# Opening an encoder layer: the modulation by quarters instead of halves, w_in tiles split in two pieces, and turns of the identity on TensorE

## The chip, the cores and the metric

One core of one Trainium2 chip runs the whole layer in one launch. The metric is the device time of one execution in microseconds (us), median of several runs. Engines: TensorE (PE), VectorE (DVE), ScalarE (ACT), GpSimd (POOL), SyncE (SP, which issues most DMAs). PE's records come in two kinds, matmuls (a transpose is one, with the identity as the second operand) and weight loads (PEld).

## The reference, cut to what matters

One layer of an encoder over 1024 prompt rows and 32 sample rows of 1024 channels, all in float32. The change concerns the beginning:

```
ada = silu(c) @ w_ada + b_ada          # c: one row for the prompt, one for the sample
sh1, sc1, gt1, sh2, sc2, gt2 = split(ada, 6)
h = rms_norm(x, g_pre_mix) * (1 + sc1) + sh1
p = h @ w_in                            # 4256 columns: latents, q, k, v of branch B, two gates
```

Behind it come two kinds of attention (multi-head latent, and stick-breaking with a strict causal mask), gated and projected, and a feed-forward part with a causal convolution. Outputs are the rows y and the new cache rows and states.

## The kernel before, in words

Everything that PE multiplies has channels on the partitions, so the rows of x are transposed on their way in. `stage_h` (L335) makes h = shift + gain * normalised x in that form, as two parts, a rounded value hh (Hht) and a remainder hl (Hlt); a product with w_in is then three matmuls per tile of 128 channels, hh x wh, hl x wh and hh x wl (`mm3`, L72 to L74), where wh and wl are the same split of a weight tile (`hi` on ACT, L65; `lo` on DVE, L68). A w_in tile is 1024 channels x 128 columns, loaded by `wload` (L82). `w_in_tile` (L388) hands out a tile that was made ahead, if there is one in `in_w`.

`load` in `stage_h` brings one block of 128 rows (x), ACT sums its squares (L105), POOL makes the reciprocal root (L97, L98) and DVE scales the rows (L345). There are eight such blocks, and one tile xs with the 32 sample rows, laid as 128 partitions x 256 channels (`quarters`); its reciprocal root needs a matmul across partitions (`rstd_s`, L320 to L324).

Shift and scale of the first part are 2 x 1024 columns of w_ada. `ada_half` (L241) makes them for 512 channels: eight k-tiles of 128 input channels, each a DMA of 512 KB (L250) and four matmuls (L253) whose stationary operand is the silu of the two c rows, padded to 32 columns, so that four of them stand side by side in PE's columns; each streams 256 columns of w_ada. In the trace each counts as two PE instructions, so a k-tile is x8. The sums go to SBUF (L255), two transposes (L258, here called the turn) put channels on partitions, the bias is added (L261), and `gain` (L237) makes g * (1 + scale). Only then can ACT make h.

`norm_T` (L266) transposes four x blocks of one k-tile (128 channels) into one PSUM bank (L282), ACT writes f = gain * x + shift (L288), DVE makes hh (a cast, L291) and hl (L292). For blocks 4 to 7 and the first half of the channels, ACT writes hh too (`both`), and DVE casts nothing. The branch for sample rows (from L296) transposes xs anew at each call.

The order in `stage_h`: blocks 0 to 3, ada half 0, norm of blocks 0 to 3; mask; the first w_in tile (q, column 672); blocks 4 to 7; the second w_in tile (k); norm of blocks 4 to 7; the sample rows; ada half 1; and the second half of the channels for all. The engines' orders are worked out by a scheduler when the program is built: it takes each instruction by its data, its engine and its priority, so that transposes, ada k-tiles and w_in matmuls of the first q and k tile (`sb_pair`, L408, over three column blocks of 352) are mixed on PE. The order thus comes from the built program, not from the text of the code. Pools set what can be ahead: wada holds 8 buffers of w_ada tiles and of x, W holds 2 w_in tiles each raw, wh and wl; PSUM has eight banks, s (3), pv (1), tr (2), mm (2).

After the last w_in matmul of the first q and k tiles, the k tile is turned back to rows (`to_natural`, L404).

Of the kernel before, what the change touches and what calls it, by code (L numbers as in the profile page):

```python
# [8 lines left out]
F32 = mybir.dt.float32  # L9
F32R = mybir.dt.float32r  # L10
BF16 = mybir.dt.bfloat16
AF = mybir.ActivationFunctionType
ALU = mybir.AluOpType
# [4 lines left out]
P = 128  # L18
D = 1024
KT = 8  # L20
# [24 lines left out]
class K:  # L45
# [192 lines left out]
            out[:, k], self.adaT[:, v, k], 1.0, self.gvT[:, g0 + k0 : g0 + k0 + n].unsqueeze(2).broadcast_to([P, n, 2]),  # L238
            ALU.add, ALU.mult)

    def ada_half(self, hf, wp, tp):  # L241

        nc, a = self.nc, self.a
        acc = self.tl(tp, [P, 256], F32, f"ada{hf}")
        ps = self.bank("s")
        for k in range(KT):

            last = hf == 1 and k >= KT - 2
            w = self.tl(*((self.W, [P, 1024]) if last else (wp, [P, 2 * 512])), F32, "wr").rearrange("p (v n) -> p v n", v=2)
            nc.sync.dma_start(w, a["w_ada"][0, k * P : (k + 1) * P].rearrange("p (v h n) -> p v h n", v=6, h=2)[:, 0:2, hf])  # L250
            for j in range(4):
                c = (j % 2) * 256
                nc.tensor.matmul(ps[32 * j : 32 * j + 32, :256], self.cT[:, k], w[:, j // 2, c : c + 256],  # L253
                                 start=k == 0, stop=k == KT - 1)
        nc.vector.tensor_copy(acc, ps[:, :256])  # L255
        tr = self.bank("s")
        for c in range(2):
            nc.tensor.transpose(tr[:, c * P : c * P + P], acc[:, c * P : c * P + P], self.idt)  # L258
        for c in range(2):
            k = slice(4 * hf + c, 4 * hf + 4, 2)  # L260
            nc.vector.tensor_tensor(self.adaT[:, 0:2, k],  # L261
                                    tr[:, c * P : c * P + P].rearrange("p (v j r) -> p v j r", v=2, j=2)[:, :, :, 0:2],
                                    self.bT[:, :, k].unsqueeze(3).broadcast_to([P, 2, 2, 2]), ALU.add)
        self.gain(self.g1, 1, 0, 4 * hf, 4)


    def norm_T(self, t0, xs, g, sv, tp, k0=0, k1=KT):


        nc = self.nc  # L270
        if t0 < 8:
            n = len(xs) * P
            m = 512 // n
            c = slice(t0 * P, t0 * P + n)
            for k in range(k0, k1, m):
                tr = self.bank("tr")
                f = self.tl(tp, [P, 512], F32, "hf").rearrange("p (k c) -> p k c", k=m)
                for e in range(m):
                    kc = slice((k + e) * P, (k + e) * P + P)
                    for j, x in enumerate(xs):  # L280
                        o = e * n + j * P
                        nc.tensor.transpose(tr[:, o : o + P], x[:, kc], self.idt)  # L282
                h, l = self.Hht[:, k : k + m, c], self.Hlt[:, k : k + m, c]

                both = t0 == 4 and k0 == 0
                for e in range(m):
                    for x in (f, h) if both else (f,):
                        nc.scalar.activation(x[:, e], tr[:, e * n : e * n + n], AF.Identity,  # L288
                                             bias=self.adaT[:, sv, k + e, 0:1], scale=g[:, k + e, 0:1])
                if not both:  # L290
                    nc.vector.tensor_copy(h, f)  # L291
                nc.vector.tensor_tensor(l, f, h.bitcast(F32), ALU.subtract)  # L292
        else:
            tr = self.bank("tr")
            for c in range(2):
                nc.tensor.transpose(tr[:, c * P : c * P + P], xs[0][:, c * P : c * P + P], self.idt)  # L296
            f = self.tl(tp, [P, 512], F32, "hf")[:, :256].rearrange("p (k t) -> p k t", t=TS)
            for k in range(k0, k1):
                j, c = k // 2, k % 2
                nc.scalar.activation(f[:, k], tr[:, c * P + 32 * j : c * P + 32 * j + 32],  # L300
                                     AF.Identity, bias=self.adaT[:, sv, k, 1:2], scale=g[:, k, 1:2])
            f, h, l = (x[:, k0:k1] for x in (f, self.Hht[:, :, TP:T], self.Hlt[:, :, TP:T]))
            nc.vector.tensor_copy(h, f)
            self.lo(l, f, h)
# [29 lines left out]
    def stage_h(self):  # L334
        nc = self.nc  # L335
        self.new_H()
        a = self.a
        with self.tc.tile_pool(name="st_h", bufs=2, reuse_waits="tile") as tp, self.tc.tile_pool(name="wada", bufs=8, reuse_waits="tile") as wp:
            self.ada_prep(tp)
            xts = []  # L340

            def load(t):
                x = self.tl(wp, [P, D], F32, "x")
                nc.sync.dma_start(x, a["x_prompt"][0, t * P : (t + 1) * P])
                nc.vector.tensor_scalar(x, x, self.rstd(self.sumsq(x, P, tp, "jk0", 1024), D, P), None, ALU.mult)  # L345
                xts.append(x)

            def norm(t, hf):
                self.norm_T(t, xts[t : t + 4] if t < 8 else [xs], self.g1, 0, tp, 4 * hf, 4 * hf + 4)

            for t in range(4):
                load(t)
            self.ada_half(0, wp, tp)
            norm(0, 0)
            mk = self.tl(tp, [P, 272], F32, "mk")
            nc.gpsimd.dma_start(mk, a["k_mask"][:, P:])
            nc.vector.tensor_copy(self.msk, mk)
            w = [self.w_in_tile(672)]
            for t in range(4, 8):
                load(t)  # L360
            w.append(self.w_in_tile(672 + 512))
            self.in_w = w
            norm(4, 0)
            xs = self.tl(tp, [P, 256], F32, "xs")
            self.quarters(xs, a["x_sample"][0], nc.gpsimd)
            nc.gpsimd.dma_start(self.sel, a["k_sel"])
            self.ada_half(1, wp, tp)
            nc.vector.tensor_scalar(xs, xs, self.rstd_s(xs, tp), None, ALU.mult)
            norm(0, 1)
            norm(8, 0)  # L370
            norm(4, 1)
            norm(8, 1)


    def mtile(self, wh, wl, xh, xl, blocks, nk, tags="mm"):
# [1351 lines left out]
    def part(self, s, i):  # L1727
        return [x[:, 512 * i : 512 * i + 512].rearrange("p (k c) -> p k c", k=4) for x in s]
# [554 lines left out]
```

## Time and profile before

| | us |
|---|---|
| median of 3 runs | 1734.95 (1734.91 to 1735.09) |
| profiled execution | 1733.42 |
| its span (first to last instruction) | 1731.7 |
| PE busy, matmuls | 1691.4 |
| DVE, ACT, POOL busy | 1249.7, 994.5, 274.6 |
| mean granted clock of PE | 0.997 |

The profile is of one execution, slightly shorter than the median of the runs; 1.7 us lie around its span. "PE busy" is time in which a matmul is under way by its record; records overlap, as the array is a pipeline, so the pitch from one start to the next says more on a matmul's cost than its duration. A row of the timeline has the start, the busy time of the group, the engine and line, the operation, out<-in by the program's names, shapes, the count, and in brackets the idle time just before and what ended it. A row of the windows has the stretch, its length, busy time (and number of instructions) of PE, PEld, DVE, ACT and POOL, then the clock granted to PE as a share of full speed, the share of the DMA engines in use, and GB/s.

### The profile page before, as it was taken

Reading aid. Unit: us, or ns where it says so; the run is one execution under the profiler, and the core shown is the slowest. Engines: PE = TensorE matmul, PEld = TensorE weight load, DVE = VectorE, ACT = ScalarE, POOL = GpSimd, SP = SyncE. Lnnn points to the kernel's source line nnn. Section 1 sums busy time; section 2 is a strip of 40 time slices with the busy share of each in tenths; the row PEclk is TensorE's granted clock in tenths of the full one; section 3 lists DMA queues with packets and bytes.
Section 4 is the critical chain, followed back from the end, with each engine's and each line's share of the span. In section 5 each row is a group of like instructions: output and inputs, shape, how many; then the busy total and the mean of one; then the engine's idle time right before and its main releaser. Section 6 shows DMA issues by size and latency. Waiting matters only on the chain. (4 is left out here: it accounts for less than half of the span.)

```text
span 1731.7 us, 29842 instructions
## 1 busy us (share of the span) xinstructions
PE 1691.4 (98%) x11546; PEld 1540.8 (89%) x11546; DVE 1249.7 (72%) x2104; ACT 994.5 (57%) x1943; POOL 274.6 (16%) x521
## 2 busy tenths in 40 slices
PE   6999999999999999999999999999999999999998
PEld 3999998999999989989888779999999999977886
DVE  4696594693873587768785678877787787788456
ACT  4595694683872677767774277444454444544442
POOL 2211111111110011101100042221111111210013
PEclk9999999999999999999999999999999999999999
DMA  9343333333332222122245631524323323697743
GB/s 325 97 126 96 107 120 85 114 105 92 113 114 54 71 79 65 61 75 68 95 170 180 190 131 41 164 97 135 129 92 128 128 92 129 204 339 248 242 147 122
DMA packets 170142, 223.78 MB, mean 129 GB/s; under 512 B 12933, under 2 KB 117072, under 8 KB 170000
## 3 DMA queue, kind: packets, MB, share of 16 engines
q1 hardware_dynamic: 154336, 177.91, 32.5%
q0 software_dynamic: 15440, 43.88, 7.2%
q8 instruction: 91, 1.49, 0.3%
q14 instruction: 51, 0.42, 0.1%
q10 hardware_dynamic: 224, 0.09, 0.0%
HBM read 170.06 MB, written 51.25 MB: 128 GB/s over the span
## 5 line engine op out<-in xcount | busy, mean ns | idle before, releaser
L65 ACT ACTIVATE wh<-wr 128x1024 fp32r<-128x1024 f32 (+6 forms) x161 | 134.3, 844 | 252.1 <-PE s L1737 80.0
L68 DVE TENSOR_TENSOR wl<-wr,wh 128x1024 fp32r<-128x1024 f32 (+6 forms) x161 | 154.4, 967 | 148.0 <-ACT wh L65 147.7
L72 PE MATMUL mm<-hh,wh 128*128 128x352 f32 x696 | 231.7, 333 | 2.8 <-ACT nat L861 2.8
L73 PE MATMUL mm<-hl,wh 128*128 128x352 f32 x696 | 226.8, 326 | 0.4 <-DVE hl L292 0.4
L74 PE MATMUL mm<-hh,wl 128*128 128x352 f32 x696 | 225.8, 324 | 0.0
L72 PEld LDWEIGHTS mm<-hh,wh 128*128 128x128 f32 x696 | 131.2, 189 | 10.5 <-ACT nat L861 4.8
L73 PEld LDWEIGHTS mm<-hl,wh 128*128 128x128 f32 x696 | 131.4, 189 | 3.2 <-DVE hl L292 1.1
L74 PEld LDWEIGHTS mm<-hh,wl 128*128 128x128 f32 x696 | 131.5, 189 | 0.4 <-issue 0.4
L1738 PE MATMUL s<-T,wl 128*128 128x256 f32 (+1 forms) x328 | 93.6, 285 | 0.0
L1737 PE MATMUL s<-T,wh 128*128 128x256 f32 (+1 forms) x328 | 93.4, 285 | 0.0
L1736 PE MATMUL s<-T,wh 128*128 128x256 f32 (+1 forms) x328 | 93.3, 284 | 0.0
L1877 DVE SCALAR_TENSOR_TENSOR u<-u,c,u 128x1058 f32<-128x1058 f32 x68 | 87.0, 1317 | 1.9 <-ACT u L1874 0.7
L603 PE MATMUL tr<-c,A 128*128 128x128 f32 x576 | 83.4, 275 | 1.5 <-DVE PTl L68 0.8
L1736 PE MATMUL tr<-T,wh 128*128 128x272 f32 (+1 forms) x272 | 77.7, 286 | 0.0
L1738 PE MATMUL tr<-T,wl 128*128 128x272 f32 (+1 forms) x272 | 77.6, 285 | 0.0
L1737 PE MATMUL tr<-T,wh 128*128 128x272 f32 (+1 forms) x272 | 77.3, 284 | 0.0
L68 DVE TENSOR_TENSOR PTl<-tr,PTh 128x512 fp32r<-128x512 f32 x100 | 67.2, 683 | 11.9 <-ACT PTh L65 11.4
L603 PEld LDWEIGHTS tr<-c,A 128*128 128x128 f32 x576 | 66.4, 140 | 9.6 <-DVE PTl L68 1.7
L68 DVE TENSOR_TENSOR wl<-S,wh 128x1024 fp32r<-128x1024 f32 x40 | 48.9, 1223 | 35.0 <-ACT wh L65 35.0
L1738 PE MATMUL mm<-T,wl 128*128 128x256 f32 (+1 forms) x256 | 72.9, 286 | 0.3 <-DVE wl L68 0.2
L1736 PE MATMUL mm<-T,wh 128*128 128x256 f32 (+1 forms) x256 | 73.0, 285 | 0.0
L1737 PE MATMUL mm<-T,wh 128*128 128x272 f32 (+1 forms) x256 | 72.7, 284 | 0.0
(689 smaller groups left out, 5519.4 us busy)
## 6 DMA issues: line engine op xcount, KB each, us to landing
wr<-in_w_ada_dram SPq DMA_DIRECT2D x48, 512.0 KB, 4.4
wr<-in_w_up_dram SPq DMA_DIRECT2D x44, 512.0 KB, 4.5
dr<-in_w_down_dram SPq DMA_DIRECT2D x43, 512.0 KB, 6.4
wr<-in_w_in_dram SPq DMA_DIRECT2D x33, 512.0 KB, 4.8
wr<-gdn SPq DMA_DIRECT2D x30, 512.0 KB, 4.2
gdn<-u POOLq DMA_DIRECT2D x23, 512.0 KB, 5.2
gd<-nat POOLq DMA_DIRECT2D x48, 176.0 KB, 2.2
t<-gd SPq DMA_DIRECT2D x16, 528.0 KB, 6.0
```

The costliest lines, as they stand in the source:

```text
L65: self.nc.scalar.activation(out, in_, AF.Identity, scale=scale)
L68: return self.nc.vector.tensor_tensor(out, full, hi.bitcast(F32), ALU.subtract)
L72: m(ps, lh, rh, start=start, stop=False)
L73: m(ps, lh, rl, start=False, stop=False)
L74: self.pe = m(ps, ll, rh, start=False, stop=stop).ins
L603: self.nc.tensor.transpose(tr[:, (2 * s + q) * P : (2 * s + q + 1) * P], at[q][:, b * P : b * P + P], self.idt)
L1736: m(ps[:, :n], w[0][:, k], x[0][:, k, c], start=first and k == 0, stop=False, skip_group_check=True)
L1737: m(ps[:, :n], w[0][:, k], x[1][:, k, c], start=False, stop=False, skip_group_check=True)
L1738: i = m(ps[:, :n], w[1][:, k], x[0][:, k, c], start=False, stop=k == 3, skip_group_check=True)
L1877: nc.vector.scalar_tensor_tensor(y, u[:, w : w + YW], self.cvT[:, w, cc : cc + 1], y, ALU.mult, ALU.add)
```

## The change

The first part of ada is made in four quarters of 256 channels instead of two halves. A quarter has eight DMAs of 256 KB (pieces of 1 KB instead of 2 KB) and 8 x 4 matmuls of 128 columns, one transpose as its turn, and its sums lie in the one bank of pv instead of s. The order is: blocks 0 to 3, quarter 0, their norm for its two k-tiles; q weight tile; blocks 4 to 7; k weight tile; their norm for quarter 0; the sample rows, transposed once and kept (xT); then for quarters 1 to 3: ada and the norms of all rows.

The two w_in tiles are split in two pieces: 256 columns (the first two k-tiles) first, the other 768 after the norm of blocks 4 to 7.

ACT no longer writes hh for blocks 4 to 7; DVE casts as for the others.

`keep_busy` issues transposes of the identity into a bank that nobody reads: 15 after quarter 0's turn, and 5 each after the transposes of blocks 4, 5 and 6 in the second k-tile of quarter 0 (the table STANDS).

```
-    def ada_half(self, hf, wp, tp):
+    def keep_busy(self, ins, n):
+        for i in range(n):
+            with self.tc.issue_after(ins):
+                ins = self.nc.tensor.transpose(self.idle[:, i % 4 * P : i % 4 * P + P], self.idt, self.idt).ins
+
+    STANDS = {(4, 1, 0): 5, (4, 1, 1): 5, (4, 1, 2): 5}
+
+    def ada_quarter(self, q, wp, tp):
...
-        acc = self.tl(tp, [P, 256], F32, f"ada{hf}")
-        ps = self.bank("s")
-        for k in range(KT):
...
+        acc = self.tl(tp, [P, P], F32, "ada")
+        ps = self.bank("pv")
+        for kk in range(KT // 2):
...
+            for e in range(2):
+                k = 2 * kk + e
+                nc.sync.dma_start(w[:, e], a["w_ada"][0, k * P : (k + 1) * P].rearrange("p (v h n) -> p v h n", v=6, h=4)[:, 0:2, q])
+                for j in range(4):
+                    c = (j % 2) * P
+                    nc.tensor.matmul(ps[32 * j : 32 * j + 32, :P], self.cT[:, k], w[:, e, j // 2, c : c + P],
+                                     start=k == 0, stop=k == KT - 1)
+        nc.vector.tensor_copy(acc, ps[:, :P])
+        tr = self.bank("pv")
+        m = nc.tensor.transpose(tr[:, :P], acc, self.idt)
+        if q == 0:
+            self.keep_busy(m.ins, 15)
...
+        self.gain(self.g1, 1, 0, 2 * q, 2)
...
-                        nc.tensor.transpose(tr[:, o : o + P], x[:, kc], self.idt)
+                        ins = nc.tensor.transpose(tr[:, o : o + P], x[:, kc], self.idt).ins
+                        if k0 == 0 and (t0, k, j) in self.STANDS:
+                            self.keep_busy(ins, self.STANDS[t0, k, j])
...
-                both = t0 == 4 and k0 == 0
...
+            def opening_tile(c0):
+                raw = self.wload([(0, 1024, a["w_in"][0, :, c0 : c0 + P].rearrange("(k p) c -> p k c", p=P), 8)])
+                h, l = (self.tl(self.W, [P, 1024], F32R, g) for g in ("wh", "wl"))
+                def part(c):
+                    self.hi(h[:, c], raw[:, c])
+                    self.lo(l[:, c], raw[:, c], h[:, c])
+                part(slice(0, 256))
+                self.in_w.append([t.rearrange("p (k c) -> p k c", k=8) for t in (h, l)])
+                return lambda: part(slice(256, 1024))
+
+            self.idle = self.bank("s")
             for t in range(4):
                 load(t)
-            self.ada_half(0, wp, tp)
+            self.ada_quarter(0, wp, tp)
             norm(0, 0)
...
+            rest = [opening_tile(672)]
+            for t in range(4, 8):
+                load(t)
+            rest.append(opening_tile(672 + 512))
+            norm(4, 0)
+            for part in rest:
+                part()
...
+            xs, xT = self.tl(tp, [P, 256], F32, "xs"), self.tl(tp, [P, 256], F32, "xT")
...
+            for c in range(2):
+                nc.tensor.transpose(tr[:, c * P : c * P + P], xs[:, c * P : c * P + P], self.idt)
+            nc.vector.tensor_copy(xT, tr[:, :256])
             norm(8, 0)
-            norm(4, 1)
-            norm(8, 1)
+            for q in range(1, 4):
+                self.ada_quarter(q, wp, tp)
+                for t in (0, 4, 8):
+                    norm(t, q)
```

In the changed kernel the matmuls of ada stand at L264, the turn at L268, the turns of the identity at L245, the transposes of x at L292, the sample rows' at L396, and `to_natural`'s at L434.

More of the change, by code (lines that the diff above doesn't have):

```diff
@@ L239, in gain @@
             ALU.add, ALU.mult)
-    def ada_half(self, hf, wp, tp):
-        nc, a = self.nc, self.a
-        acc = self.tl(tp, [P, 256], F32, f"ada{hf}")
-        ps = self.bank("s")
-        for k in range(KT):
[L248 to L264, printed above, removed]
@@ new lines, in keep_busy @@
+    def keep_busy(self, ins, n):
[4 more added lines that the diff above has]
+    def ada_quarter(self, q, wp, tp):
+        nc, a = self.nc, self.a
+        acc = self.tl(tp, [P, P], F32, "ada")
+        ps = self.bank("pv")
+        for kk in range(KT // 2):
+            last = q == 3 and kk == KT // 2 - 1
+            w = self.tl(*((self.W, [P, 1024]) if last else (wp, [P, 1024])), F32, "wr").rearrange("p (e v n) -> p e v n", e=2, v=2)
+            for e in range(2):
[10 more added lines that the diff above has]
+            self.keep_busy(m.ins, 15)
+        k = slice(2 * q, 2 * q + 2)
+        nc.vector.tensor_tensor(self.adaT[:, 0:2, k], tr[:, :P].rearrange("p (v j r) -> p v j r", v=2, j=2)[:, :, :, 0:2],
+                                self.bT[:, :, k].unsqueeze(3).broadcast_to([P, 2, 2, 2]), ALU.add)
+        self.gain(self.g1, 1, 0, 2 * q, 2)
@@ L276, in norm_T @@
                 tr = self.bank("tr")
-                f = self.tl(tp, [P, 512], F32, "hf").rearrange("p (k c) -> p k c", k=m)
+                f = self.tl(tp, [P, 512], F32, "hf")[:, : m * n].rearrange("p (k c) -> p k c", k=m)
                 for e in range(m):
@@ L281, in norm_T @@
                         o = e * n + j * P
-                        nc.tensor.transpose(tr[:, o : o + P], x[:, kc], self.idt)
+                        ins = nc.tensor.transpose(tr[:, o : o + P], x[:, kc], self.idt).ins
+                        if k0 == 0 and (t0, k, j) in self.STANDS:
+                            self.keep_busy(ins, self.STANDS[t0, k, j])
                 h, l = self.Hht[:, k : k + m, c], self.Hlt[:, k : k + m, c]
-                both = t0 == 4 and k0 == 0
                 for e in range(m):
[L287 to L291, printed above, removed]
+                    nc.scalar.activation(f[:, e], tr[:, e * n : e * n + n], AF.Identity,
+                                         bias=self.adaT[:, sv, k + e, 0:1], scale=g[:, k + e, 0:1])
+                nc.vector.tensor_copy(h, f)
                 nc.vector.tensor_tensor(l, f, h.bitcast(F32), ALU.subtract)
         else:
-            tr = self.bank("tr")
-            for c in range(2):
-                nc.tensor.transpose(tr[:, c * P : c * P + P], xs[0][:, c * P : c * P + P], self.idt)
+            tr = xs[0]
+            if tr.shape[1] == 256 and k1 - k0 == KT:
+                tr = self.bank("tr")
+                for c in range(2):
+                    nc.tensor.transpose(tr[:, c * P : c * P + P], xs[0][:, c * P : c * P + P], self.idt)
             f = self.tl(tp, [P, 512], F32, "hf")[:, :256].rearrange("p (k t) -> p k t", t=TS)
@@ L346, in load, with norm @@
                 xts.append(x)
-            def norm(t, hf):
-                self.norm_T(t, xts[t : t + 4] if t < 8 else [xs], self.g1, 0, tp, 4 * hf, 4 * hf + 4)
+            def norm(t, q):
+                self.norm_T(t, xts[t : t + 4] if t < 8 else [xT], self.g1, 0, tp, 2 * q, 2 * q + 2)
+            def opening_tile(c0):
[8 more added lines that the diff above has]
+            self.idle = self.bank("s")
             for t in range(4):
                 load(t)
-            self.ada_half(0, wp, tp)
+            self.ada_quarter(0, wp, tp)
             norm(0, 0)
+            self.in_w = []
+            rest = [opening_tile(672)]
[5 more added lines that the diff above has]
+                part()
             mk = self.tl(tp, [P, 272], F32, "mk")
@@ L357, in stage_h @@
             nc.vector.tensor_copy(self.msk, mk)
[L358 to L364, printed above, removed]
+            xs, xT = self.tl(tp, [P, 256], F32, "xs"), self.tl(tp, [P, 256], F32, "xT")
             self.quarters(xs, a["x_sample"][0], nc.gpsimd)
             nc.gpsimd.dma_start(self.sel, a["k_sel"])
-            self.ada_half(1, wp, tp)
             nc.vector.tensor_scalar(xs, xs, self.rstd_s(xs, tp), None, ALU.mult)
-            norm(0, 1)
+            tr = self.bank("tr")
+            for c in range(2):
+                nc.tensor.transpose(tr[:, c * P : c * P + P], xs[:, c * P : c * P + P], self.idt)
+            nc.vector.tensor_copy(xT, tr[:, :256])
             norm(8, 0)
-            norm(4, 1)
-            norm(8, 1)
+            for q in range(1, 4):
+                self.ada_quarter(q, wp, tp)
+                for t in (0, 4, 8):
+                    norm(t, q)
     def mtile(self, wh, wl, xh, xl, blocks, nk, tags="mm"):
```

## The prediction

> **What bounds the kernel now.** I read the page first (busy time of each engine over the span), then the stretches of the opening with the granted clock, then the order of TensorE's work, and last what ACT and DVE did just ahead of its idle places.
>
> ```profile
> PE 1691.4 (98%) x11546; PEld 1540.8 (89%) x11546; DVE 1249.7 (72%) x2104; ACT 994.5 (57%) x1943; POOL 274.6 (16%) x521
> ```
>
> TensorE (PE) is occupied for 98% of the 1731.7 us span: about 40 us are idle, and the change can win only idle time, half-clock time, or work of PE's. In the built program PE's order is the same in both kernels from the first transposes L404 on, behind the first Q and K tiles; call this point the join. What happens to the join happens to the end, one for one, as PE is full behind it. The opening in stretches (second column length, then PE busy; then the clock and the DMA share):
>
> ```profile
> 20.00:25.00 5.00, 1.89 (x18) 0.78 (x14) 2.18 (x6) 2.44 (x4) 0.00 (x0) 1.00 1.08 370
> 25.00:30.00 5.00, 3.36 (x12) 2.32 (x12) 3.57 (x7) 5.00 (x9) 2.93 (x6) 0.61 1.07 359
> 30.00:35.00 5.00, 4.16 (x21) 2.61 (x20) 4.20 (x7) 2.76 (x6) 1.30 (x3) 0.71 1.05 383
> 35.00:40.00 5.00, 4.88 (x44) 3.01 (x45) 2.77 (x4) 4.48 (x9) 0.00 (x0) 1.00 0.95 352
> 40.00:45.00 5.00, 4.45 (x50) 2.83 (x49) 1.19 (x6) 0.00 (x0) 0.74 (x2) 1.00 0.11 16
> ```
>
> So the hole is between 20 and 35 us: 5.6 us idle, and the clock at half for a part. The places on PE:
>
> ```profile
> 20.81 0.64 PE L253 MATMUL s<-wr,cT 128*32 128x256 f32 x8 [0.65 <-DMA wr<-in_w_ada_dram]
> 22.00 0.44 PE L258 MATMUL s<-c,ada 128*128 128x128 f32 x2 [0.55 <-DVE ada L255]
> 24.34 0.33 PE L282 MATMUL tr<-c,x 128*128 128x128 f32 x1 [1.90 <-ACT hf L288]
> ...
> 25.42 0.41 PE L72 MATMUL mm<-hh,wh 128*128 128x352 f32 x1
> ...
> 28.36 0.45 PE L282 MATMUL tr<-c,x 128*128 128x128 f32 x1 [0.33 <-ACT hf L288]
> ...
> 44.24 0.44 PE L258 MATMUL s<-c,ada 128*128 128x128 f32 x2 [0.55 <-DVE ada L255]
> ...
> 67.82 0.71 PE L404 MATMUL tr<-c,big 128*128 128x128 f32 x5
> ```
>
> The last ada k-tile of half 0 is at 20.81, its turn at 22.00, the first w_in matmul at 25.42, the first transpose of rows 4 to 7 at 28.36, the second turn at 44.24, the join at 67.82.
>
> **The change, part by part.**
>
> *The start.* Half 0 needs 4 MB of w_ada ahead of the first turn, quarter 0 needs 2 MB. By the DMA rate of the stretch 25 to 30 (359 GB/s) 2 MB are 5.8 us, so data alone would put the last k-tile at 15.0. PE's other work sets a later bound:
>
> ```profile
> 11.38 1.08 PE L253 MATMUL s<-wr,cT 128*32 128x256 f32 x8 [2.25 <-DMA wr<-in_w_ada_dram]
> ...
> 16.64 0.69 PE L282 MATMUL tr<-c,x 128*128 128x128 f32 x2
> 22.75 0.17 DVE L237 SCALAR_TENSOR_TENSOR c<-c,c 128x8 f32<-128x8 f32 x1
> 22.56 1.06 ACT L65 ACTIVATE wh<-wr 128x1024 fp32r<-128x1024 f32 x1 [11.43 <-DMA wr<-in_w_in_dram]
> 23.52 0.76 ACT L288 ACTIVATE hf<-tr,c,c 128x512 f32<-128x512 f32 x1
> ```
>
> The fourth x tile's transposes (16.64, end 17.3) stay where they are; in the built order one or two k-tiles of quarter 0 follow, .54 each if half of 1.08, so the last begins near 17.4. From the last k-tile to the gain were 22.92 - 20.81 = 2.1 us: gain at **19.5** instead of 22.92. Behind it ACT did the whole first weight split (1.06) before hf; now w_in lands earlier and only 256 columns are split first. The chain from gain to the first w_in matmul was 25.42 - 22.92 = 2.5; without the split in its way about 1.8: first w_in at 21.3. The rows 4 to 7 follow in the same ACT and DVE chain, so their first transpose moves from 28.36 to about **25.2: -3.2 us**. This is what the change earns.
>
> *Count of PE's work from there to the join.* Both have 138 w_in matmuls left. Before: 48 transposes L282, 4 L296, 8 ada k-tiles, one turn. After: 56 transposes, 2 for the sample rows, 24 ada k-tiles of half the columns, three turns, and 15 turns of the identity behind x4's, x5's and x6's transposes. Prices, at full clock:
>
> ```profile
> 37.47 0.32 PE L73 MATMUL mm<-hl,wh 128*128 128x352 f32 x1
> 37.72 0.64 PE L253 MATMUL s<-wr,cT 128*32 128x256 f32 x8
> 38.28 0.43 PE L74 MATMUL mm<-hh,wl 128*128 128x352 f32 x1
> 38.55 0.32 PE L72 MATMUL mm<-hh,wh 128*128 128x352 f32 x1
> 38.71 0.32 PE L73 MATMUL mm<-hl,wh 128*128 128x352 f32 x1
> ...
> 40.10 1.07 PE L282 MATMUL tr<-c,x 128*128 128x128 f32 x8
> 41.10 0.64 PE L253 MATMUL s<-wr,cT 128*32 128x256 f32 x8
> ...
> 42.19 1.50 PE L253 MATMUL s<-wr,cT 128*32 128x256 f32 x24
> ```
>
> A w_in matmul is .16 (38.71 - 38.55); 8 transposes are 1.00, so .12 each with the change-over and about .11 in stream. Of the ada k-tiles three in a row took 1.50, one alone .64: (1.50 - .64) / 2 = **.43 in stream**. One put alone between w_in matmuls costs more: from 37.47 to 38.55 stand two w_in (.32) and one k-tile in 1.08, so .76, that is **.33 on top for going in and out**. In the trace the 8 k-tiles of half 1 stand in 6 places: 8 x .43 + 6 x .33 = 5.4 us. In the built order of the changed kernel the 24 small k-tiles stand in 22 places, between other matmuls or transposes. No row shows a 128-column k-tile. Its stream lies between .22 (half) and .43 (unchanged), its in-and-out between 0 and .33. I take half the stream, as 4 turns of the same 128 columns also need .44, and the whole of the in-and-out, since that is a change of the weights' shape (128x32 against 128x128) and the columns don't enter into it: 24 x .22 + 22 x .33 = 12.5 us, **+7.1**. At the ends: no in-and-out 5.3 (-.1); no shrinking 24 x .43 + 22 x .33 = 17.6 (+12.2).
>
> *The small terms.* 8 transposes more and 2 fewer: +.7. Two turns more with their change-over: +.3. The 15 turns of quarter 0 lie between the gain's chain at 19.5 and the first w_in at 21.3, 15 x .11 = 1.7 in 1.8 us, cost 0 (at half clock, twice that, up to +1.5). The other 15 lie while PE waits for the next x tile:
>
> ```profile
> 27.46 0.75 DVE L345 TENSOR_SCALAR x<-x,rs 128x1024 f32<-128x1024 f32 x1 [0.72 <-POOL rs L98]
> 28.93 0.75 DVE L345 TENSOR_SCALAR x<-x,rs 128x1024 f32<-128x1024 f32 x1 [0.71 <-POOL rs L98]
> ```
>
> The x tiles come 1.47 apart; five turns (.55) and two transposes (.22) fit: cost 0, without that cover 1.7. From 28.36 to 32.62 the trace lost time there at half clock too; at full clock the wait for x takes its place, since DVE and POOL don't follow PE's clock. So I count nothing there; the stall behind it does go:
>
> ```profile
> 33.62 0.78 ACT L288 ACTIVATE hf<-tr,c,c 128x512 f32<-128x512 f32 x1 [2.24 <-PE tr L282]
> 34.30 0.77 ACT L288 ACTIVATE hh<-tr,c,c 128x512 fp32r<-128x512 f32 x1
> PE tr L282 <- ACT hh L288: 0.9, 1, 0.9
> ```
>
> ACT wrote each of four blocks twice (hf, hh), .67 apart, and PE stood .9 for it; now DVE does the second: -.9, and near -1 more from matmuls of this stretch that then run at full clock. Against it a new wait: the sample rows are transposed once (L396) ahead of most ada work, and the scale that they need went through this chain:
>
> ```profile
> 39.96 0.28 PE L322 MATMUL tr<-ss,c 128*128 128x1 f32 x2
> 40.27 0.16 DVE L324 COPY tot<-tr 128x1 f32<-128x1 f32 x1 [0.46 <-PE tr L322]
> 41.38 0.35 DVE L368 TENSOR_SCALAR xs<-xs,rs 128x256 f32<-128x256 f32 x1 [0.94 <-POOL rs L98]
> ```
>
> From L322 on PE (39.96) to xs (41.73) are 1.8 us, of which PE's built order covers about 1: +.8, queued behind it on PE is quarter 1. Sum of the small: +.7 +.3 -.9 -1 +.8 = **-.1**, between -1.5 and +2.
>
> *At nothing:* 32 DMAs of 256 KB for 16 of 512 KB on SP's queue. The DMA share falls to .11 after 40 us, and PE reaches quarter 3 only at 46 or later; cover 4 to 6 us. A tile's second 768 columns need one more ACT pass (about .45 fixed) and are used from quarter 1 on. Bank pv has one buffer: a quarter's first matmul waits for the read of the last turn, .24 as in L261's pair; behind it only other quarters' work, and w_in matmuls stand between.
>
> **Sum:** -3.2 + 7.1 - .1 = +3.8, and the join was 67.82. Where a k-tile's neighbour is a transpose, the first matmul after it loses less (8 transposes at .12 each with the change-over): I take .05 off at some ten of 22 places, -.5. **+3.3 us**, join near 71.1. Of the profiled 1733.42 that makes 1736.7; the median of the runs is 1734.95, 1.5 above the profiled one, and so the forecast is **1738.2**. A measurement can tell about 0.2%, 3.5 us, from no change.
>
> **The rivals.**
>
> *A, the clock isn't held.* Before, the clock was raised and lowered in steps of 3.41 us:
>
> ```profile
> 15.85:19.27 3.42, 3.42 (x30) 1.29 (x26) 0.00 (x0) 0.00 (x0) 0.00 (x0) 1.00 1.05 388
> 19.27:22.68 3.41, 1.96 (x26) 0.60 (x18) 0.63 (x3) 0.12 (x1) 0.00 (x0) 1.00 1.10 342
> 22.68:26.09 3.41, 1.47 (x9) 1.00 (x9) 2.64 (x7) 3.41 (x6) 0.00 (x0) 1.00 1.03 412
> 26.09:29.51 3.42, 2.28 (x6) 1.56 (x6) 1.99 (x4) 3.42 (x7) 2.52 (x5) 0.50 1.08 338
> 29.51:32.92 3.41, 3.18 (x11) 2.43 (x11) 3.34 (x7) 1.87 (x3) 1.71 (x4) 0.50 1.05 386
> ```
>
> After a stretch with 1.96 busy of 3.41 the clock stayed; after 1.47 it fell; after 2.28 at half clock it was not raised; after 3.18 it was. If the identity turns count as work, a stretch with them is as full as the first row and the clock is at full from about 22.7; that is in the forecast. If they don't, the holes stay empty and full clock comes only at 29.5 or 32.9. From 25 on PE has some 2.4 us of full-clock work per step, at half clock 4.8 in 3.4: 1.1 to 2.4 us lost, join +4.4 to +5.7, 1739.3 to 1740.6. Chance .18.
>
> The Trainium skill, "TensorE: Matmul & The Clock Gate", Part 4, says that the full clock does not engage for transpose mode, as it "doesn't count as PE-busy the same way". By that rule A would hold. No run here shows turns of the identity alone, so the trace decides neither for nor against it.
>
> *B, faster.* The in-and-out of a small k-tile is hidden: its weights (32 columns) load while the neighbours stream. For it speaks that the three k-tiles at 42.19 stream without a gap; against it every single insertion of the trace, .64 busy and .43 for the matmul after it. Then the ada term is -.1 and the sum -3.2 -.1 -.1 = -3.4, and with a start half a microsecond better -4: 1731. It decides from .18 per place down (22 x .15 = 3.3, the gain eaten). Chance .10.
>
> *C, the small k-tiles don't shrink.* Each group of four 32-column weights takes its time whatever streams. +12.2 in place of +7.1: +8.4, 1743.3. Half of it +5.8, 1740.8. Chance .14.
>
> *D, no difference.* The in-and-out is about half (.17), as the last matmul's lengthened record is partly overlap: the sum is +3.3 - 22 x .16 = -.2 to +1.5, 1734.8 to 1736.5. This is also the case in which the change doesn't do what it says, opening early but giving it back. Chance .20.
>
> **How the numbers follow.** Forecast .38 (+1.5 to +5), A .18, B .10, C .14, D .20. Faster by over 0.2%: B, .10. Within: D, half the forecast (+1.5 to +3.5) and a little of A: .42. Slower: half the forecast, A and C: .48. The range leaves out half of B and of C: 1733 to 1742.5.
>
> **What would show it.** The first w_in matmul near 21.3 and x4's transposes near 25.2: if not earlier than 25.42 and 28.36, the start is wrong. L264's k-tiles alone near .54 from matmul to matmul: at .22 B, at .76 C. The third and fourth turns near 46.6 and 54.6; the join near 71. The clock record: a fall behind 22.7 is A. The prediction fails at large if the order behind the join doesn't run as before, or if PE waits for w_ada in quarters 1 to 3.

## The result, and the profile after

The changed kernel takes **1737.49 us** (median of 22 runs, 1734.82 to 1738.94) against 1735.03 for the kernel before (22 runs, 1731.96 to 1739.49). The ratio is 1.0013, with a 95% interval of 1.0007 to 1.0019, that is 1.2 to 3.3 us slower: clear of noise, but inside the 0.2% that the prediction called no difference. The forecast was 1738.2.

The page after, and PE's order at the same places (start, busy time, line, then what ended the idle time):

```profile
span 1736.5 us, 30189 instructions
## 1 busy us (share of the span) xinstructions
PE 1700.3 (98%) x11702; PEld 1548.3 (89%) x11702; DVE 1252.1 (72%) x2119; ACT 992.4 (57%) x1941; POOL 270.7 (16%) x521
```

```profile
17.46 1.08 PE L264 MATMUL pv<-wr,cT 128*32 128x128 f32 x16
18.96 0.47 PE L268 MATMUL pv<-c,ada 128*128 128x128 f32 x1 [0.41 <-DVE ada L266]
19.23 3.29 PE L245 MATMUL s<-c 128*128 128x128 f32 x15
22.27 0.41 PE L72 MATMUL mm<-hh,wh 128*128 128x352 f32 x1
...
25.56 0.64 PE L292 MATMUL tr<-c,x 128*128 128x128 f32 x2 [1.75 <-DVE x L355]
...
46.84 0.27 PE L268 MATMUL pv<-c,ada 128*128 128x128 f32 x1
...
54.77 0.27 PE L268 MATMUL pv<-c,ada 128*128 128x128 f32 x1
...
71.65 0.71 PE L434 MATMUL tr<-c,big 128*128 128x128 f32 x5
```

PE is busy for 9 us more, with 156 instructions more (the 30 turns of the identity, 128 from the smaller k-tiles, two transposes of sample rows fewer). The first turn is at 18.96 instead of 22.00, the first w_in matmul at 22.27 instead of 25.42, the transposes of block 4 at 25.56 instead of 28.36: the opening does start some 3 us earlier. By the join (the transposes L434, L404 before) that is all lost: 71.65 against 67.82, 3.8 us later. Between the two stand the small k-tiles. One of them, alone between w_in matmuls:

```profile
45.63 0.32 PE L73 MATMUL mm<-hl,wh 128*128 128x352 f32 x1
45.89 0.42 PE L264 MATMUL pv<-wr,cT 128*32 128x128 f32 x8
46.24 0.43 PE L74 MATMUL mm<-hh,wl 128*128 128x352 f32 x1
46.51 0.32 PE L72 MATMUL mm<-hh,wh 128*128 128x352 f32 x1
```

From 45.63 to 46.51 stand two w_in matmuls (.16 each) and one k-tile: it costs .56 for half the columns, where the whole one cost .76.

The clock in steps of 3.41 us (the share granted is the number just ahead of the last two). One thing has to be known to read it: ahead of a trace's first clock record this column shows 1.00 whatever the clock was. The first record after is a rise at 22.26, and the pitch of 15 turns in 3.04 us (19.23 to 22.27, .20 each, against .11 at full clock) says that PE ran at half until then. The same goes for the stretch 15.85 to 19.27 in the prediction's quote.

```profile
18.85:22.26 3.41, 3.30 (x16) 3.31 (x17) 1.87 (x7) 2.33 (x4) 0.00 (x0) 1.00 1.02 405
22.26:25.68 3.42, 1.66 (x9) 1.00 (x8) 2.53 (x4) 3.42 (x8) 1.82 (x4) 1.00 1.13 324
25.68:29.09 3.41, 3.41 (x17) 3.13 (x18) 1.51 (x2) 1.93 (x4) 3.07 (x5) 0.50 1.08 345
29.09:32.50 3.41, 3.37 (x38) 2.07 (x36) 3.28 (x6) 1.49 (x3) 0.03 (x1) 1.00 1.09 348
```

The first step holds the turn and the identity turns, and the clock rises at its end. The second has the hole ahead of block 4 (1.75 us idle), and the clock falls. The third is filled by turns and transposes, and the clock rises again.

The transfers also got slower: from 30 to 35 and 35 to 40 us the trace shows 348 and 347 GB/s where before showed 383 and 352, and they end later. PE didn't wait for it: its waits show one entry between 20 and the join:

```profile
PE tr L292 <- DVE x L355: 1.7, 1, 1.7
```

### The profile page after: what moved, and what is told of

Same layout as the page of the kernel before. It is cut to its first block, busy times and chain, and to the rows that moved or that the text cites. A ratio compares the mean times of both kernels' runs of the same rounds, so it can differ in the third digit from the quotient of the medians.

```text
span 1736.5 us, 30189 instructions
## 1 busy us (share of the span) xinstructions
PE 1700.3 (98%) x11702; PEld 1548.3 (89%) x11702; DVE 1252.1 (72%) x2119; ACT 992.4 (57%) x1941; POOL 270.7 (16%) x521
## 3 DMA queue, kind: packets, MB, share of 16 engines
q1 hardware_dynamic: 158688, 177.91, 32.7%
```

## The experiments

**Theory:** the change loses on PE, by .33 us for each place where a small k-tile interrupts other matmuls; the earlier start is worth about 3 us, and the turns of the identity ("the turns" from here on) cost nothing. **Rivals:** the small k-tiles cost their time wherever they stand; or the turns cost more than they bring; or the split of w_in decides. All kernels, with the times of the opening from one profile each. A ratio is to runs of the kernel before that were taken beside it; their medians were 1735.03 for the changed kernel, 1734.43 for the packs of eight and of two, no turns and w_in split whole, and 1735.38 for the other four:

| kernel | places of ada's k-tiles, quarters 1 to 3 | first w_in | join | median us | ratio to before, 95% |
|---|---|---|---|---|---|
| before | 6 (half 1) | 25.42 | 67.82 | 1735.03 | |
| changed | 22 | 22.27 | 71.65 | 1737.49 | 1.0007 to 1.0019 |
| packs of eight | 3 | 21.60 | 69.04 | 1734.22 | .9991 to 1.0010 |
| packs of two | 13 | 22.18 | 69.26 | 1734.95 | .9995 to 1.0013 |
| changed, no turns | 22 | 21.67 | 76.75 | 1742.02 | 1.0024 to 1.0055 |
| changed, w_in split whole | 24 | 22.23 | 72.34 | 1738.39 | 1.0012 to 1.0035 |
| before, with turns | 6 (half 1) | 25.43 | 69.31 | 1733.85 | .9989 to 1.0007 |
| changed, 15 turns only | 22 | 21.54 | 75.94 | 1743.25 | 1.0033 to 1.0060 |
| packs, late second pieces | 5 | 21.61 | 67.83 | 1733.15 | .9979 to .9996 |
| before, turns and packs of four | 2 (half 1) | 25.39 | 68.67 | 1734.87 | .9990 to 1.0008 |

**Packs of eight.** The k-tile whose data come last is multiplied first, so that all eight stand together.

```
+        G = 1 if q == 0 else 8
+        ws = []
...
-                for j in range(4):
-                    c = (j % 2) * P
-                    nc.tensor.matmul(ps[32 * j : 32 * j + 32, :P], self.cT[:, k], w[:, e, j // 2, c : c + P],
-                                     start=k == 0, stop=k == KT - 1)
+                ws.append((k, w[:, e]))
+                if len(ws) < G:
+                    continue
+                for i, (kt, we) in enumerate(ws[-1:] + ws[:-1]):
+                    for j in range(4):
+                        c = (j % 2) * P
+                        nc.tensor.matmul(ps[32 * j : 32 * j + 32, :P], self.cT[:, kt], we[:, j // 2, c : c + P],
+                                         start=k == G - 1 and i == 0, stop=k == KT - 1 and i == G - 1)
+                ws = []
```

> The changed kernel, but in quarters 1 to 3 the eight k-tiles of ada wait for the last one's data and then stand together on PE: 3 places instead of 22. Theory (going in and out of a small k-tile costs .33 us per place): 19 places fewer, 6.3 us, the join falls from 71.65 to 65.4 (66.5 at most if PE waits for data of w_ada), and the time to about 1731.3, 3.7 below before. Rival (a small k-tile costs its .5 us wherever it stands): join within .5 of 71.65, time as the changed kernel, 1737.5.

The join is 69.04: 2.6 us earlier, not 6.3. Theory and rival both missed. PE's order shows what a pack costs, and PE's waits from 20 us to the join show the rest (total, times, longest):

```profile
36.32 1.95 PE L270 MATMUL pv<-wr,cT 128*32 128x128 f32 x64
38.21 0.43 PE L72 MATMUL s<-hh,wh 128*128 128x352 f32 x1
```

```profile
PE tr L299 <- DVE x L362: 3.1, 4, 1.8
PE tr L299 <- ACT hf L304: 0.8, 1, 0.8
PE tr L403 <- issue: 0.5, 1, 0.5
PE mm L72 <- DVE hh L306: 0.4, 1, 0.4
PE mm L74 <- DVE wl L68: 0.2, 1, 0.2
```

Eight k-tiles take 1.95 and one alone .42, so one in stream is (1.95 - .42) / 7 = .22, half of the .43 of the large one; an isolated place then costs .56 - .22 = .34.

The waits sum to 5.0 us, against 1.7 in the changed kernel. Not all of these 3.3 are gain that was lost: 1.3 lie between blocks 4 and 7, where the clock here was at full (from 21.10 on) and PE waited, while in the changed kernel the turns ran at half clock and took up the same time. The transposes of block 7, first here, then in the changed kernel:

```profile
29.77 0.44 PE L299 MATMUL tr<-c,x 128*128 128x128 f32 x2 [0.33 <-DVE x L362]
```

```profile
29.96 0.44 PE L292 MATMUL tr<-c,x 128*128 128x128 f32 x2
```

From there to the join both kernels have the same work and full clock: 39.3 us here, 41.7 there. 1.8 of the 39.3 are waits (ACT's hf, DVE's hh, and one put down to issue), none of the 41.7. So PE's work shrank by 2.4 + 1.8 = 4.2 us for 19 places, .22 for each. A place has a price, then, but taking it away gives back less than the .34 of an isolated one. A likely reason is that many k-tiles stand beside transposes, which keep a change-over of their own against the w_in matmuls; that isn't shown. The waits that remain point to the rows of blocks 4 to 7 and to quarter 1's channels, whose gain now comes behind all eight k-tiles.

**Packs of two.** The same with G = 2.

> The same with pairs: 13 places instead of 22. Theory: 9 x .33 = 3.0 us less, join 68.7, time about 1734.5, no difference from before. Rival: join within .5 of 71.65. If the gain per place falls with the number taken away, the price isn't one of the place.

Join 69.26, 2.4 us earlier for 9 places, .27 for each, while its clock rose 1.1 us later than in the changed kernel (23.32 and 30.15). From block 7's transposes (30.21) it is 39.05 us against 41.69, with no wait in either: .29 for each. Close to the theory's .33 and far from the rival's nothing; the time, 1734.95, isn't told from before, as expected. The gain per place does fall with the number taken away, from .29 (9 places) to .22 (19), so the price isn't the same for every place.

**No turns.** `keep_busy` does nothing.

```
-        for i in range(n):
+        for i in range(0):
```

> The changed kernel without its 30 turns of the identity. Theory (turns count as work for the clock): without them no step of 3.41 us between 18.8 and 29.1 is full, the clock stays at half until 29.1 or 32.5, PE loses up to half of a step from 29.1 on: join 71.6 to 73.3, more likely 73.3. Rival (turns don't hold the clock, the w_in matmuls do): the same clock record as with turns, and a join of 71.2 to 71.65.

Join 76.75, 5.1 us later, beyond what either side gave. The clock's first record is the rise at 43.13. The pitch shows half clock until there and full clock behind it:

```profile
31.56 0.50 PE L74 MATMUL s<-hh,wl 128*128 128x352 f32 x1
31.86 0.50 PE L72 MATMUL s<-hh,wh 128*128 128x352 f32 x1
32.15 0.50 PE L73 MATMUL s<-hl,wh 128*128 128x352 f32 x1
...
45.38 0.33 PE L72 MATMUL s<-hh,wh 128*128 128x352 f32 x1
45.55 0.60 PE L292 MATMUL tr<-c,x 128*128 128x128 f32 x4
```

From 31.56 to 32.15 the pitch is .30, from 45.38 to 45.55 .17. The theory was right that the turns count as work for the clock, and wrong on how long it would take without them.

**15 turns only.** The table STANDS is empty; the 15 behind quarter 0 stay.

```
-    STANDS = {(4, 1, 0): 5, (4, 1, 1): 5, (4, 1, 2): 5}
+    STANDS = {}
```

> The changed kernel with the 15 turns behind quarter 0 only, without the 3 x 5 between the x blocks. Theory: the first 15 raise the clock at about 22.3, the step behind it is nearly empty and it falls again, and what follows doesn't raise it, as without any turns: join 75 to 77 (near 72 only if the steps of 3.41 us happen to fall so that none is empty). Rival (the first 15 do it all): join 71.2 to 71.8 in any case.

Join 75.94: as the theory had it. The first turns raised the clock at 20.88, it fell at 27.70, and rose again only at 41.36. Its stretches behind 29 us:

```profile
29.20:32.70 3.50, 3.01 (x23) 1.78 (x22) 3.25 (x7) 1.74 (x3) 0.00 (x0) 0.50 1.09 348
32.70:36.10 3.40, 3.40 (x29) 1.62 (x21) 0.61 (x1) 0.22 (x2) 0.00 (x0) 0.50 1.10 348
36.10:39.50 3.40, 3.40 (x18) 2.50 (x18) 0.51 (x2) 0.00 (x0) 0.74 (x2) 0.50 0.90 290
```

PE is on record as busy throughout from 32.7 to 39.5, and the clock stays at half (from 38.62 to 38.91 the pitch of w_in matmuls is .29). So the 15 turns between the blocks are what brings the clock back at 29.09 in the changed kernel. Ahead of the mix with small k-tiles that is worth more than in the kernel before, whose clock was back for good without any turns at 32.92, 34.03 and 34.58 in its three profiles.

**w_in split whole.**

```
-                part(slice(0, 256))
+                part(slice(0, 1024))
...
-                return lambda: part(slice(256, 1024))
+                return lambda: None
```

> The changed kernel with the two w_in tiles split whole, 1024 columns at once. Theory (the start is set by quarter 0's gain, and ACT does hf ahead of the weight anyway): the first w_in matmul moves by under .5 us, the first transposes of rows 4 to 7 not at all, join within .4 of 71.65. Rival (the first 256 columns are what lets PE start early): first w_in 1 us later, join 72.5 or more.

The first w_in is at 22.23 and block 4's transposes at 25.47, both unmoved, as expected; the third w_in matmul waited .88 us for wl, inside the hole ahead of block 4. The join is 72.34, .7 later than in the changed kernel's first profile and .2 later than in its second (below): more than expected. The order on PE is another one, with the small k-tiles in 24 places, as two of quarter 1's are cut in two by other work; two places more account for .4 to .7. The rival's late start isn't there, but the run is a weak test of it: wh was ready at 22.17 (21.12 + 1.05), just when the turns at half clock let go of PE. And in the changed kernel ACT makes both pieces of a tile one behind the other (21.27 and 21.57; 26.47 and 26.77), ahead of the h of blocks 4 to 7 (30.33) and not around it, as the program's text has them. The run also says that the half clock is not what the changed kernel loses by: here the clock was at full from 22.92 through the join, which came no earlier.

**Before, with the turns.** The turns are put at the same places into `ada_half` and `norm_T` of the kernel before, in a bank of mm.

```
+        if hf == 0:
+            self.keep_busy(m.ins, 15)
...
+                        if k0 == 0 and (t0, k, j) in self.STANDS:
+                            self.keep_busy(ins, self.STANDS[t0, k, j])
```

> The kernel before, with only the 30 turns of the identity added: 15 behind half 0's turn, 5 each behind the transposes of blocks 4 to 6 of the second k-tile. Theory (turns count as work for the clock, and lie in holes): the half clock from 26.1 to 32.9 goes, six w_in matmuls and some five transposes at half speed there cost 1.4 us less, but the x blocks still come 1.47 apart: join 66.3 to 67.3 instead of 67.82, time .5 to 1.5 below before. Rival (turns cost their 30 x .11 us on PE, the clock is nothing): join 69 to 71.

Join 69.31, 1.5 later, inside the rival's 69 to 71; the time isn't told from before (.9989 to 1.0007). Its clock rose at 17.19, fell at 30.84 and rose at 34.25, so half clock took 3.4 us instead of 6.8, and it brought nothing. In its order five turns stand at half clock from 31.38 to 32.31, directly ahead of a w_in matmul, and PE still waits 1.08 for a block at 29.76.

**Before, with turns, and half 1 in packs of four.** The edit of the packs, with 256 columns and G = 4 for half 1.

> The kernel before with the 30 turns, and half 1's eight k-tiles (256 columns) in two packs of four: 2 places instead of 6. Theory: 4 x .33 = 1.3 us less than with the turns alone, join 65 to 66, time 2 to 2.8 below before. Rival (packing starves PE of half 1's channels as it starved the packed quarters): join no better than with the turns alone.

Join 68.67, with the clock at full from 17.95 to the end. Against the turns alone the join is .6 earlier instead of 1.3, the time not told from before: the rival more than the theory. PE's waits point to why even a full clock and fewer places gain next to nothing here (6.3 us in all, 5.4 with the turns alone):

```profile
PE tr L300 <- ACT hh L308: 1.4, 1, 1.4
PE tr L300 <- ACT hf L308: 1.2, 2, 1.0
PE s L274 <- DVE ada L271: 1.1, 2, 0.5
PE tr L300 <- DVE x L365: 1.1, 1, 1.1
PE s L268 <- DMA wr<-in_w_ada_dram: 0.8, 1, 0.8
PE mm L73 <- DVE hl L312: 0.7, 2, 0.4
```

With a start at 25.4 the kernel before waits for ACT and for the blocks, and a PE that is done sooner waits longer.

**Packs, with late second pieces.** Quarter 1 in two packs of four, quarters 2 and 3 in packs of eight, and ACT makes the 768-column pieces behind the h of blocks 4 to 7.

```
+        G = (1, 4, 8, 8)[q]
...
-            for part in rest:
-                part()
+            with self.tc.issue_after(self.hf_ins):
+                for part in rest:
+                    part()
```

> As the eight together, but quarter 1 in two packs of four, and ACT splits the second pieces of w_in (768 columns) only behind the h of blocks 4 to 7. Theory (the packed kernel lost 3.4 us to idle PE, as blocks 4 to 7 and quarter 1's gain come too late for it): blocks 4 to 7 come .7 earlier, quarter 1's gain 1 to 2 earlier, join 67.5 to 68.3 instead of 69.04, time near 1733. Rival (the idle time only moves, for the sample rows' chain gets .4 later): join 68.7 to 69.4.

Join 67.83, and 1733.15 us: **.9979 to .9996 of before**, faster by .7 to 3.6 us, and with that faster than the changed kernel (1.0007 to 1.0019). Block 4's transposes came at 24.58 (25.36 in the packs of eight), quarter 1's turn at 37.63 (38.80).

```profile
24.58 0.44 PE L299 MATMUL tr<-c,x 128*128 128x128 f32 x2 [0.89 <-DVE x L362]
...
37.63 0.33 PE L275 MATMUL pv<-c,ada 128*128 128x128 f32 x1
...
67.83 0.71 PE L442 MATMUL tr<-c,big 128*128 128x128 f32 x5
```

Its waits sum to 3.9 us where the packs of eight had 5.0:

```profile
PE tr L299 <- DVE x L362: 2.2, 4, 0.9
PE mm L72 <- ACT wh L65: 0.7, 1, 0.7
PE mm L72 <- DVE hh L306: 0.4, 1, 0.4
PE tr L404 <- issue: 0.4, 1, 0.4
PE mm L74 <- DVE wl L68: 0.2, 1, 0.2
```

Its clock was at full from 18.30 on, in the packs of eight from 21.10; the first w_in matmul came at the same time in both (21.61 and 21.60), so that is at most a small part of its join. Two things were changed at once, and what each is worth was not tried. So opening by quarters is of use, once the k-tiles are taken together and the second pieces held back.

**How much one profile says.** The two kernels once more, unchanged, one profile and one time each.

> The kernel before, unchanged, one more profile. Theory (the steps of the clock fall anew in each execution, and the join goes with them): other steps, and a join that differs from 67.82 by .5 to 2 us. Rival (the opening is the same each time, and the spread of the times comes from behind the join): 67.82 within .3.

> The changed kernel, unchanged, one more profile. Theory: other steps of the clock, a join between 70.5 and 73. Rival: 71.65 within .3.

> The kernel before, a third profile, for the same question: theory a join between 66.5 and 70, rival 67.82 within .3.

Before: 68.59 and 67.91 (with 67.82, a mean of 68.1). Changed: 72.12 (with 71.65, 71.9). The steps of the clock fell anew each time (first rise at 16.96 and 17.51; 17.60), so the theory holds in kind, but the join moved by .1 to .8 only, less than expected. The single times of these three are 1736.88, 1733.17 and 1738.94. The 3.8 us between the kernels stand.

## Why the prediction was right, step by step

- **The bound.** PE's order behind the join did not change, and PE is still at 98%. "One for one" is not shown: the join is 3.8 us later, the median 2.46 (1.2 to 3.3), and the two profiled executions differ by 4.8 (1733.42 and 1738.23). From the join to the last matmul the first profiles have 1656.7 (before) and 1657.7 (after), the eleven other profiles of this study 1654.5 to 1659.7; such shifts of 2 us in either direction hide where a microsecond goes, and whether one is taken up behind the join stays open. The forecast of +3.3 put the join at 71.1, .5 too early, and the whole of it into the time, .8 too much.
- **The start.** Gain at 19.83 (19.67 + .16) where 19.5 was said; first w_in 22.27 for 21.3. Some .6 of that is the 15 turns, which ran at half clock up to 22.27 and held PE, the case named with up to +1.5: without turns it came at 21.67. In the second profile, with full clock from 17.60, it is at 21.30. The step behind the gain ran in another order than said: ACT wrote hf twice first and the 256 columns of wh behind it, and the first w_in waited for wh where the turns didn't hold it (21.30 in the second profile, 21.67 without turns). The forecast length of 1.8 came out at 1.9 (19.40 to 21.30 in the second profile), with another chain. Block 4 at 25.56 for 25.2: -2.8 instead of -3.2.

```profile
19.67 0.16 DVE L237 SCALAR_TENSOR_TENSOR c<-c,c 128x4 f32<-128x4 f32 x1
...
19.93 1.45 ACT L297 ACTIVATE hf<-tr,c,c 128x512 f32<-128x512 f32 x2 [8.52 <-DVE c L237]
21.27 1.14 ACT L65 ACTIVATE wh<-wr 128x256 fp32r<-128x256 f32 x2
```

- **The k-tiles.** The term that decides was right in both parts for the isolated k-tile: .22 in stream (the packs), .34 per place (.33 said), .56 alone (.55 said). For the sum: from 30.33 to 54.45 PE's order has the 24 k-tiles among 39 w_in matmuls and 46 other instructions; at the prediction's prices for these (.16, and .11 to .12 for a transpose) and with .3 idle they leave 12.2 to 12.6 us, .31 to .33 per place, against 12.5, or 12.0 with the .5 taken off for neighbours. Against the 5.4 of before that is +6.8 to +7.2. It includes what short runs of transposes cost beyond that price, which may be why the packs gave back only .22 to .29 per place. The third and the fourth quarter's turn stand at 46.84 and 54.77 where 46.6 and 54.6 were said. Rival C (no shrinking) is out. Rival B (hidden) is out by every single insertion.
- **The turns.** Counted at nothing, and with them in place that holds. But without them the kernel is 5.1 us later at the join, where the loss of the clock (rival A) was priced at 1.1 to 2.4: the term that was mis-sized most, though it wasn't called on. The first of A's rows, 15.85 to 19.27, stands at 1.00 but was at half clock, so it shows a step that raised the clock and not one that kept it. Part of A did come: the clock fell at 25.68 for one step. It cost little, for PE waits there for the blocks.

  The Trainium skill, "TensorE: Matmul & The Clock Gate", Part 4, has the full clock not engage for transpose mode, which doesn't count as work in the same way. The step from 18.85 to 22.26 holds the turn and 15 identity turns, the one from 25.68 to 29.09 only turns and transposes, and the clock rose behind both: these traces disagree with that rule for the transposes of this kernel (the trace calls them MATMUL and doesn't show a mode).
- **The small terms.** With -2.8 for the start and +6.8 to +7.2 for the k-tiles, the join's +3.8 leaves -.6 to -.2 for the rest, where -.1 was said. The stall of .9 behind the doubled ACT writes is gone, as said. The sample rows' wait was priced at .8; PE's waits have no entry for it, and the gap ahead of their transposes, from 35.32 to 35.78, is .3 after the matmul's .16. The DMAs of half size cost nothing, though the rate fell.
- **D, no difference,** is out by the join, +3.8 where it had +1.5 at most, and by the isolated place, .34 where it had .17; the .22 that the packs of eight gave back lies between the two. Its upper end (1736.5) is 1 us short of the time. What is measured lies in the forecast's own range, +1.5 to +5, in the half of it that was counted as no difference, and the terms stand behind it: the sum didn't come out by errors that cancel, as start, k-tiles and the rest are each within .6 of what was said.

## What to carry to other kernels

Cutting a transfer's consumer in smaller pieces to start earlier also cuts PE's work into more places; if each piece is another shape of weights, count the places in the built order and price them by one isolated insertion in the trace before counting the head start. Expect less than that price back when the places go (here .2 to .3 of .34). Then let the pieces that aren't needed early stand together, and see what PE waits for when it is no longer the bound. A few transposes of the identity can be worth far more than their own time where PE's work doesn't get the clock (5.1 us of the opening in the changed kernel), and bring nothing elsewhere (the kernel before).

## What the runs showed of the hardware that was not expected

- The clock stayed at half while PE was on record as busy without a gap: 32.7 to 39.5 us with 15 turns only, and 32.90 to 43.13 without turns. In the kernel before, the step from 29.51 to 32.92 with 3.18 us busy was enough. The difference between these steps is the mix: w_in matmuls cut by single 128-column k-tiles in the one, w_in and plain transposes in the other. The step that ended in the rise at 43.13 had no w_in matmul at all, but three k-tiles between transposes, so it isn't the k-tiles alone that keep the clock down. Which part of an instruction's time counts was not tried and stays open.

  The Trainium skill, "TensorE: Matmul & The Clock Gate", Part 1, has full clock after about 3.4 us of sustained work; by the records of PE's busy time the stretches above disagree.
- Turns of the identity alone are enough to raise it: at 22.26 behind the first 15, after a step (18.85 to 22.26) in which PE did nothing else but the one turn of quarter 0.
